# Block sums of the down projection's weights staged through DRAM, and thirteen pairs of k-tiles by Strassen's scheme

## Chip, cores and metric

One core of one Trainium2 chip runs the whole layer as one program. The metric is the device time of one execution in microseconds (us): 1745.18 us, the median of three runs of the kernel before (1744.41 to 1745.37).

## What is computed

A layer of depth 1 over 256 tokens of width 2048, in float32: a norm, a wide input projection, three branches (a gated convolution, a chunked linear recurrence, attention to 256 memory rows), an output projection with residual, and a feed-forward part. The change concerns the last matrix product:

```python
act = gelu(causal_dwconv3(up_g, conv_ffn_w) + conv_ffn_b) * up_v     # 256 x 5632
ffn_out = einsum('bsf,fd->bsd', act, w_ffn_down)                     # 5632 x 2048
x = x + rms_norm(ffn_out, norm_ffn_post)
```

## The kernel before

Every float32 operand is split in a rounded part and a rest (`wh` and `wl` of a weight, two halves of an activation tile), and a product is made of three matmuls: high by high, high by low, low by high. Weights come in tiles of 128 x 2048 (1 MiB) that SP's queue loads into three buffers named `w`. A tile is worked in units of 1024 columns, here called halves. For each, ScalarE casts `wh` (L1025, in the down projection L820) and VectorE subtracts to get `wl` (L1026, L821); there are four buffers of each. The main loop (L1118) walks about 600 units in order: the first 16 are the lead tiles, which carry the memory rows beside weights, then the key and value weights of the memory (`wkvT`, `wkvN`), then the input projection (`winT`, `winN`), the branches, `wout`, the up projection, the down projection. It prepares up to three units ahead and calls `bg(1)`, one step of background work, per unit. The instructions are then ordered by a list scheduler with its own idea of when an engine is free, except where `pin` or a raised priority holds them, so an instruction may stand on its engine far from its unit.

The down projection (`down_units`, `column_pair`) goes through two pairs of 512-column groups (p = 0 and 1), each over 22 pairs of k-tiles j. An ordinary pair, E below, takes 8 products in two units (`run_eight`). A pair in `SEVEN`, S below, takes 7 products by Strassen's scheme in Winograd's form in four units (`run_seven`): it needs sums of blocks of the activations, made in the up projection (`sums_of_operand`), and sums of blocks of the weights, which VectorE makes for every such pair (L840, L842, L843 in `load_seven`) in a quarter of the tile `down`. Ten of 22 pairs are S, alternating with E. `combine` folds the shared products at the last S of a column pair, and `run_shares` adds them to the accumulators for p = 1. `down` is 32 KB per partition, takes the memory of `a_x1` once the up projection is over, and also holds the results of p = 0 and the row of the last norm.

Of the kernel before, what the change touches and what calls it, by code (L numbers as in the profile page):

```python
# [16 lines left out]
P = 128  # L17
# [13 lines left out]
SEVEN = tuple(range(1, 20, 2))  # L31
FF = 4
# [29 lines left out]
def block_kernel(ctx: ExitStack, tc: tile.TileContext, xT, lead, cols, wkvT, wkvN, winT, winN, wbr, wout, wup, wlead, wdown, grow, xN, masks, out):  # L62
# [6 lines left out]
    psm = ctx.enter_context(tc.tile_pool(name="psm", bufs=4, space=bass.MemoryType.PSUM))  # L69
    phase1 = ExitStack()  # L70
# [469 lines left out]
    def mix_done(cg):  # L540
        def f(ps, tt):
# [6 lines left out]
            if tt == 0:  # L548
                st["x1"] = outer.tile([P, 2, D], F32, name="x1", tag="c16")
                st["a_x1"] = outer.tile([P, KT, 2 * T], F32R, name="a_x1", tag="a32")  # L550
# [153 lines left out]
    def sums_of_operand(j, y1, y2):  # L704
# [9 lines left out]
        a = st["act", 2 * j]  # L714
        p, q = t256("s12"), t256("s34")
        a11, a21, a12, a22 = y1[:, 0:P], y1[:, P:T], y2[:, 0:P], y2[:, P:T]
        nc.vector.tensor_tensor(p[:, 0:P], a21, a22, op=ALU.add)
        nc.vector.tensor_tensor(p[:, P:T], p[:, 0:P], a11, op=ALU.subtract)
        nc.vector.tensor_tensor(q[:, 0:P], a11, a21, op=ALU.subtract)
# [4 lines left out]

    def down_tile():
        if "down" not in st:
            st["down"] = outer.tile([P, 4, D], F32, name="down", tag="a32")
            st["ffn"], st["gf"] = st["down"][:, 0:2], st["down"][:, 2]
            nc.gpsimd.dma_start(st["gf"], grow[1].partition_broadcast(P))
# [6 lines left out]

    def down_norm(ps, tt, cg, n):
        down_tile()
        f, sums, w = st["ffn"][:, tt, cg * 512:(cg + 1) * 512], st["s3"][:, tt], st["s3w"][:, tt]
        with tc.high_priority():  # L740
            nc.scalar.activation(f, ps, AF.Square, accum_out=sums[:, n:n + 1])
            nc.vector.tensor_tensor(f, ps, st["gf"][:, cg * 512:(cg + 1) * 512], op=ALU.mult)
# [4 lines left out]
    def down_last(ps, tt, cg):  # L747
# [3 lines left out]
        x1, ffn = st["x1b"], st["ffn"][:, tt]  # L751
        hold = pin if tt else lambda op: op
        with tc.high_priority():
# [4 lines left out]
            hold(nc.scalar.activation(ffn[:, cut(cg)], ps, AF.Square, accum_out=sums[:, 3:4]))  # L758
# [3 lines left out]
            hold(nc.vector.tensor_tensor(ffn[:, cut(cg)], ps, st["gf"][:, cut(cg)], op=ALU.mult))  # L762
            hold(nc.vector.tensor_scalar(h, h, r, r, op0=ALU.mult, op1=ALU.mult))
            hold(nc.vector.tensor_scalar(r1, h, 1.5, r, op0=ALU.add, op1=ALU.mult))
            if tt:
                dg = t256("dg")[:, 0:P]
                hold(nc.scalar.activation(dg, ident, AF.Copy, scale=r1))
                hold(nc.tensor.matmul(turned, lhsT=dg, rhs=ffn[:, cut(0)], start=False, stop=True))
# [4 lines left out]
            for c, lo, hi in parts:  # L773
                f = ffn[:, c * 512 + lo:c * 512 + hi]
# [3 lines left out]

    def down_units():
        rest = [j for j in range(DP) if j not in SEVEN]
        mixed = []
        for n in range(10):
            mixed += [(rest[n], False), (SEVEN[n], True)]
        orders = [mixed + [(j, False) for j in rest[10:]]]
        mixed = []
        for n in range(9):
            mixed += [(rest[n], False), (SEVEN[n], True)] + ([(SEVEN[9], True)] if n == 4 else [])
        orders.append(mixed + [(j, False) for j in rest[9:]])  # L790
# [5 lines left out]
    def column_pair(p, order):  # L796
# [15 lines left out]
        def fetch(hold, j):  # L812
            hold["w"] = wpool.tile([P, 2048], F32, name="w", tag="w", bufs=3)
            nc.sync.dma_start(hold["w"], wdown[p * DP + j])
# [8 lines left out]
        def load_eight(hold, j, h):  # L823
            if h == 0:
                fetch(hold, j)
# [4 lines left out]
        def load_seven(hold, j, q):  # L830
            if q == 0:
                fetch(hold, j)
            w = hold["w"]
            if q < 2:
                wh, wl, low = halve(w[:, 1024:2048] if q == 0 else w[:, 0:512])
                low()
                return wh, wl
            t13, t24 = down_tile()[:, 3, 0:1024], down_tile()[:, 3, 1024:2048]
            if q == 2:
                nc.vector.tensor_tensor(t13, w[:, 512:1536], w[:, 0:1024], op=ALU.subtract)  # L840
                wh, wl, low = halve(t13)
                nc.vector.tensor_tensor(t24[:, 0:512], w[:, 1024:1536], t13[:, 0:512], op=ALU.subtract)  # L842
                nc.vector.tensor_tensor(t24[:, 512:1024], w[:, 1536:2048], t24[:, 0:512], op=ALU.subtract)  # L843
                low()
                return wh, wl
            wh, wl, low = halve(t24)
            low()
            return wh, wl
# [4 lines left out]
        def share(b):  # L853
            return st["down"][:, 3, shares[b] * 512:(shares[b] + 1) * 512]

        def load_shares(h):
            wh, wl, low = halve(st["down"][:, 3, h * 1024:(h + 1) * 1024])
# [8 lines left out]
        def combine():  # L866
            u = st["down"][:, 3].rearrange("p (a b) -> p a b", a=4)
            with tc.high_priority():
                nc.scalar.copy(u[:, 0], bank["P6"])
                nc.vector.tensor_tensor(u[:, 0], bank["P1"], u[:, 0], op=ALU.add)  # L870
                nc.scalar.copy(u[:, 1], bank["P7"])
                nc.vector.tensor_tensor(u[:, 1], u[:, 0], u[:, 1], op=ALU.add)
                nc.scalar.copy(u[:, 3], bank["P1"])
                nc.scalar.copy(u[:, 2], bank["P5"])
                nc.vector.tensor_tensor(u[:, 0], u[:, 0], u[:, 2], op=ALU.add)
                nc.vector.tensor_tensor(u[:, 2], u[:, 1], u[:, 2], op=ALU.add)
# [321 lines left out]
```

## Time and profile before

| what | value |
|---|---|
| median of the runs | 1745.18 us |
| the profiled execution | 1745.41 us, its span 1743.6 us |
| TensorE (PE) busy | 1734.7 us, 99% of the span |
| VectorE (DVE) busy | 1317.4 us, 76% |
| ScalarE (ACT) busy | 955.4 us, 55% |
| moved by DMA | 331.62 MB, mean 190 GB/s |

The profiled execution took 1745.41 us; its span, from the first to the last instruction seen, is 1743.6 us, so 1.8 us lie around it. The granted clock of TensorE is full over the whole span. Busy time of PE is modelled, since matmuls overlap; how close PE is to its limit is better read from the number of matmuls in a stretch.

### The profile page before, as it was taken

To read this page: it belongs to the slowest core of one execution; us is meant where nothing else is said; L and a number is where in the kernel's file an instruction comes from. 1 tells how busy PE (TensorE), PEld (TensorE's weight loads), DVE (VectorE), ACT (ScalarE), POOL (GpSimd) and SP (SyncE) were. 2 spreads that over 40 slices of the span, in tenths; PEclk is the share of its full clock that TensorE was granted. 3 is DMA by queue.
4 is the path that set the end of the run, shared out by engine and by line. 5 is a ranking of instruction groups with operands and counts; after the bars stand their busy time and mean duration, and the time that the engine had idled before them with its cause. 6 is when DMAs were issued, how large, how long until landed. Compare 5 with 4: busy or idle time off the path is not lost.

```text
span 1743.6 us, 24264 instructions
## 1 busy us (share of the span) xinstructions
PE 1734.7 (99%) x9354; PEld 1492.5 (86%) x9354; DVE 1317.4 (76%) x2149; ACT 955.4 (55%) x1505; POOL 8.4 (0%) x20
## 2 busy tenths in 40 slices
PE   9999999999999999999999999999999999999998
PEld 8888888888888888888888888888888888878786
DVE  8866665477788887867675587777777777888997
ACT  7644654456555465656664474444454444556554
POOL 0000000000000000000000000000000000000000
PEclk9999999999999999999999999999999999999999
DMA  8644455554454544465555555555555555555653
GB/s 312 234 173 154 160 193 193 188 174 170 171 180 168 183 169 170 172 241 191 193 191 176 188 214 182 186 192 192 181 186 190 193 181 184 214 197 198 245 196 131
DMA packets 47843, 331.62 MB, mean 190 GB/s; under 512 B 5488, under 2 KB 6000, under 8 KB 8432
## 3 DMA queue, kind: packets, MB, share of 16 engines
q1 hardware_dynamic: 45792, 321.28, 51.5%
q0 software_dynamic: 1504, 8.39, 1.3%
q8 instruction: 73, 1.20, 0.3%
q10 hardware_dynamic: 432, 0.41, 0.1%
q14 instruction: 42, 0.34, 0.1%
HBM read 325.87 MB, written 4.19 MB: 189 GB/s over the span
## 4 chain that ended last, share of the span: by engine, by line
PE 97%; DVE 1%; DMA 1%; ACT 1%; issue 0%; SPq 0%; ACTq 0%; DVEq 0%
PE acc L1083 47%; PE acc L1084 24%; PE acc L1096 3%; PE acc L1094 3%; PE acc L1095 3%; PE sm L808 2%; PE acc L808 2%; PE sm L809 2%; PE acc L807 2%; PE acc L809 2%; PE sm L807 2%; PE sm L397 1%; PE sm L1083 1%; DVE wl L821 0%; DMA w<-wdown 0%; PE sm L302 0%
## 5 line engine op out<-in xcount | busy, mean ns | idle before, releaser
L1083 PE MATMUL acc<-a_x,wh 128*128 128x512 f32 x3072 | 1088.3, 395 | 0.9 <-DVE a_x L94 0.9
L1025 ACT CAST wh<-w 128x1024 fp32r<-128x1024 f32 (+2 forms) x517 | 539.2, 1044 | 619.0 <-PE acc L1083 367.5
L1026 DVE TENSOR_TENSOR wl<-w,wh 128x1024 fp32r<-128x1024 f32 (+2 forms) x517 | 627.1, 1213 | 321.9 <-ACT wh L1025 320.3
L1084 PE MATMUL acc<-a_x,wl 128*128 128x256 f32 x3072 | 869.9, 283 | 0.0
L1083 PEld LDWEIGHTS acc<-a_x,wh 128*128 128x128 f32 x3072 | 577.1, 188 | 131.6 <-DVE a_x L94 1.5
L1084 PEld LDWEIGHTS acc<-a_x,wl 128*128 128x128 f32 x3072 | 577.7, 188 | 0.3
L112 DVE TENSOR_TENSOR ev<-acc,ev 128x256 f32<-128x256 f32 x245 | 102.3, 418 | 0.8 <-ACT ev L111 0.8
L820 ACT CAST wh<-w 128x1024 fp32r<-128x1024 f32 x88 | 81.6, 954 | 23.3 <-PE sm L809 10.5
L821 DVE TENSOR_TENSOR wl<-w,wh 128x1024 fp32r<-128x1024 f32 x88 | 91.8, 1097 | 2.7 <-ACT wh L820 2.7
L111 ACT COPY ev<-acc 128x256 f32<-128x256 f32 x245 | 88.2, 361 | 1.4 <-PE acc L1084 1.4
L820 ACT CAST wh<-down 128x1024 fp32r<-128x1024 f32 x42 | 44.0, 1051 | 75.4 <-PE sm L809 36.9
L821 DVE TENSOR_TENSOR wl<-down,wh 128x1024 fp32r<-128x1024 f32 x42 | 51.3, 1223 | 17.1 <-ACT wh L820 16.8
L808 PE MATMUL sm<-wl,act 128*128 128x512 f32 x136 | 53.7, 395 | 0.2 <-DVE wl L821 0.2
L808 PE MATMUL acc<-wl,act 128*128 128x512 f32 x136 | 53.8, 396 | 0.0
L809 PE MATMUL sm<-wh,act 128*128 128x512 f32 x136 | 53.7, 395 | 0.0
L807 PE MATMUL acc<-wh,act 128*128 128x512 f32 x136 | 53.7, 395 | 0.0
L807 PE MATMUL sm<-wh,act 128*128 128x512 f32 x136 | 53.6, 394 | 0.0
L809 PE MATMUL acc<-wh,act 128*128 128x512 f32 x136 | 53.6, 394 | 0.0
L1096 PE MATMUL acc<-wh,a_m 128*128 128x512 f32 x128 | 50.5, 395 | 0.0
L1094 PE MATMUL acc<-wh,a_m 128*128 128x512 f32 x128 | 50.5, 395 | 0.0
L1095 PE MATMUL acc<-wl,a_m 128*128 128x512 f32 x128 | 50.5, 395 | 0.0
L1083 PE MATMUL acc<-ya,wh 128*128 128x512 f32 x128 | 46.1, 398 | 0.0
(328 smaller groups left out, 1987.7 us busy)
## 6 DMA issues: line engine op xcount, KB each, us to landing
w<-winT SPq DMA_DIRECT2D x104, 1024.0 KB, 4.8
w<-wup SPq DMA_DIRECT2D x84, 1024.0 KB, 4.8
w<-wdown SPq DMA_DIRECT2D x44, 1024.0 KB, 4.9
w<-wbr SPq DMA_DIRECT2D x24, 1024.0 KB, 4.8
w<-wout SPq DMA_DIRECT2D x16, 1024.0 KB, 4.8
w<-wkvN SPq DMA_DIRECT2D x8, 1024.0 KB, 4.8
w<-winN SPq DMA_DIRECT2D x8, 1024.0 KB, 4.8
w<-lead SPq DMA_DIRECT2D x7, 1024.0 KB, 5.2
```

The source lines that it names most:

```text
L807: nc.tensor.matmul(ps, lhsT=hi, rhs=w0_, start=b not in started, stop=False)
L808: nc.tensor.matmul(ps, lhsT=hi, rhs=w1_, start=False, stop=False)
L809: nc.tensor.matmul(ps, lhsT=lo, rhs=w0_, start=False, stop=stop)
L820: nc.scalar.copy(wh[:, 0:n], src)
L821: return wh, wl, lambda: nc.vector.tensor_tensor(wl[:, 0:n], src, wh[:, 0:n], op=ALU.subtract)
L1025: ops = (nc.scalar.copy(wh[:, cs], wsl[:, cs]), nc.vector.tensor_tensor(wl[:, cs], wsl[:, cs], wh[:, cs], op=ALU.subtract))
L1026: nc.vector.tensor_tensor(wl[:, cs], wsl[:, cs], wh[:, cs], op=ALU.subtract))
L1083: hold(nc.tensor.matmul(job.ps, lhsT=wh[:, sl], rhs=a, start=first, stop=False))
L1084: hold(nc.tensor.matmul(job.ps[:, 0:T], lhsT=wl[:, sl], rhs=a[:, 0:T], start=False, stop=last))
L1094: nc.tensor.matmul(job.ps[tt], lhsT=hi, rhs=w0_, start=kt == 0, stop=False)
L1095: nc.tensor.matmul(job.ps[tt], lhsT=hi, rhs=w1_, start=False, stop=False)
L1096: nc.tensor.matmul(job.ps[tt], lhsT=lo, rhs=w0_, start=False, stop=kt == job.nkt - 1)
```

## The change

Thirteen pairs of k-tiles instead of ten go by the scheme of seven products: j = 14, 16 and 18 (`EXTRA`) join, and `PATTERN` sets the order of E and S in each column pair. The weight sums are no longer made in the down projection. A background generator `stage` loads each of the 26 weight tiles concerned (13 pairs, two column pairs) in the first half of the program on POOL's queue, adds blocks in place on DVE (one instruction of 1024 columns, two of 512) and stores the tile, which holds three sums, to a DRAM scratch `stored`, again on POOL's queue. Two buffers serve it. It is advanced by one step at each of the units 36 to 115 and 252 to 331. In the down projection an S pair loads three quarters of its weight tile and the whole stored tile. A smaller `down` (8 KB per partition) serves as a fourth weight buffer, in turn with the three of `w`. The block sums of the activations of the three new pairs are made at the first ordinary pairs of p = 0 (`late_sums`). Signs in the scheme and the order of its units change with the new sums; the results and the norm's row lie in pieces of 1024 columns, the second pieces allotted after `combine` of p = 1.

```diff
-        start_norm("x", "a32", outer)
+        start_norm("x", "a32", apool)
...
+    def late_sums(n):
+        j, down = EXTRA[n], down_tile()
+        x = st["sums"][n]
+        a1, a2 = st["act", 2 * j], st["act", 2 * j + 1]
+        y1, y2 = t256("s1"), t256("s2")
+        for y, a in ((y1, a1), (y2, a2)):
+            nc.vector.tensor_tensor(y, a[:, 0:T], a[:, T:2 * T], op=ALU.add)
+        st["xs", j] = x
+        block_sums(x, a1, y1, y2)
...
+    def stage(groups):
+        tiles = {}
+        def load_(n):
+            if n < len(groups):
+                p, j = groups[n]
+                tiles[n] = ph.tile([P, 2048], F32, name="stage", tag="stage", bufs=2)
+                nc.gpsimd.dma_start(tiles[n], wdown[p * DP + j])
+        load_(0)
+        yield
+        for n, (p, j) in enumerate(groups):
+            load_(n + 1)
+            yield
+            t = tiles.pop(n)
+            nc.vector.tensor_tensor(t[:, 0:1024], t[:, 0:1024], t[:, 512:1536], op=ALU.add)
+            yield
+            for c in (1024, 1536):
+                low = 0 if c == 1024 else 1024
+                nc.vector.tensor_tensor(t[:, c:c + 512], t[:, c:c + 512], t[:, low:low + 512], op=ALU.add)
+            yield
+            stored[p, j] = dram.tile([P, 2048], F32, name=f"sums{p}_{j}")
+            nc.gpsimd.dma_start(stored[p, j], t)
+            yield
...
+        def weight_tile(pos):
+            counter["w"] += 1
+            if counter["w"] % 4 == 0 and (pos < 20 if p == 0 else 1 < pos < 18):
+                return down_tile()
+            return wpool.tile([P, 2048], F32, name="w", tag="w", bufs=3)
+
+        def fetch(hold, pos, j, seven):
+            hold["w"] = weight_tile(pos)
+            src = wdown[p * DP + j]
+            if not seven:
+                nc.sync.dma_start(hold["w"], src)
+                return
+            for cs in (slice(0, 512), slice(1024, 2048)):
+                nc.sync.dma_start(hold["w"][:, cs], src[:, cs])
+            hold["sums"] = weight_tile(pos)
+            nc.sync.dma_start(hold["sums"], stored[p, j])
...
-            if q == 2:
-                nc.vector.tensor_tensor(t13, w[:, 512:1536], w[:, 0:1024], op=ALU.subtract)
-                wh, wl, low = halve(t13)
-                nc.vector.tensor_tensor(t24[:, 0:512], w[:, 1024:1536], t13[:, 0:512], op=ALU.subtract)
-                nc.vector.tensor_tensor(t24[:, 512:1024], w[:, 1536:2048], t24[:, 0:512], op=ALU.subtract)
-                low()
-                return wh, wl
-            wh, wl, low = halve(t24)
+            w, sums = hold["w"], hold["sums"]
+            wh, wl, low = halve((w[:, 0:512], w[:, 1024:2048], sums[:, 0:1024], sums[:, 1024:2048])[q])
             low()
...
@@ -1121,6 +1189,8 @@
         multiply(n)
         load_to(n + 3)
         bg(1)
+        if any(n in r for r in STAGE):
+            next(staging[0], None)
```

Where the scheduler puts this is seen in the order of the instructions on each engine. The first place is the start of the program. On POOL, whose queue does all of the staging (`ident` is a constant), before:

```order
masks.py:197 MEMSET ident 128x128
masks.py:199 ISA
masks.py:199 AFFINE_SELECT ident<-ident 128x128
L536 DMA gp<-grow 128x2048
L538 DMA xn<-xN 128x2048 x2
```

and with the change:

```order
masks.py:197 MEMSET ident 128x128
L824 DMA stage<-wdown 128x2048
masks.py:199 ISA
masks.py:199 AFFINE_SELECT ident<-ident 128x128
L824 DMA stage<-wdown 128x2048
L839 DMA sums_1_1128<-stage 128x2048
L824 DMA stage<-wdown 128x2048
```

The first two loads, 1 MiB each, wait for nothing and stand at the very start, not at unit 36. On DVE at the same place (`a_mem` is the memory operand, `lb` constants of the recurrence), before:

```order
L245 TENSOR_TENSOR lb<-lb_e_1006 128x8
L246 TENSOR_SCALAR lb<-lb 128x8
L94 SCALAR_TENSOR_TENSOR a_mem<-w,col_sb,a_mem 128x256
L248 TENSOR_SCALAR one_m_lb<-lb 128x8
L250 TENSOR_SCALAR la<-lb 128x8
L1026 TENSOR_TENSOR wl<-w,wh 128x768
```

and with the change:

```order
L251 TENSOR_TENSOR lb<-lb_e_1013 128x8
L832 TENSOR_TENSOR stage<-stage 128x1024
L100 SCALAR_TENSOR_TENSOR a_mem<-w,col_sb,a_mem 128x256
L1094 TENSOR_TENSOR wl<-w,wh 128x768
L252 TENSOR_SCALAR lb<-lb 128x8
L836 TENSOR_TENSOR stage<-stage 128x512
L254 TENSOR_SCALAR one_m_lb<-lb 128x8
L256 TENSOR_SCALAR la<-lb 128x8
L836 TENSOR_TENSOR stage<-stage 128x512
```

The three adds of the first staged tile now stand around the work of the second lead unit, the first of them ahead of its operand.

The second place is DVE at the end of the lead units, where the statistics of the memory's norm (`sqacc`) and the first evictions (`ev`) come together. Before:

```order
L207 TENSOR_TENSOR sqacc<-msq 128x256
L1026 TENSOR_TENSOR wl<-w,wh 128x768
L102 TENSOR_SCALAR sqacc<-sm 128x256
L1026 TENSOR_TENSOR wl<-w,wh 128x1024
L104 TENSOR_TENSOR sqacc<-sqacc,rs_mem 128x256
```

and with the change:

```order
L213 TENSOR_TENSOR sqacc<-msq 128x256
L836 TENSOR_TENSOR stage<-stage 128x512
L832 TENSOR_TENSOR stage<-stage 128x1024
L108 TENSOR_SCALAR sqacc<-sm 128x256
L1094 TENSOR_TENSOR wl<-w,wh 128x1024
L836 TENSOR_TENSOR stage<-stage 128x512
L1094 TENSOR_TENSOR wl<-w,wh 128x1024
L110 TENSOR_TENSOR sqacc<-sqacc,rs_mem 128x256
```

Three adds of the second and third staged tiles stand in it now. From there on the staging is dense: all adds of the fourth to the 26th tile stand between the 34th and the 98th `wl` half of the main loop, where the code asks for a tile per four units and for a second stretch from unit 252.

The third place is SP's queue at the start of the down projection, with the change (before, it is one load of `w<-wdown` 128x2048 per pair):

```order
L886 DMA w<-wdown 128x2048
L889 DMA w<-wdown 128x512
L889 DMA w<-wdown 128x1024
L891 DMA w<-sums_1_1128 128x2048
L891 DMA w<-sums_3_1262 128x2048
L889 DMA down<-wdown 128x512
L889 DMA down<-wdown 128x1024
L886 DMA w<-wdown 128x2048
```

An S pair now takes two tiles and three loads, 1.75 MiB, and every fourth tile is `down`.

## Rows read from the trace of the kernel before

**Rows 1.** The page, parts 1 and 4: engine totals, and the chain by engine.

```profile
PE 1734.7 (99%) x9354; PEld 1492.5 (86%) x9354; DVE 1317.4 (76%) x2149; ACT 955.4 (55%) x1505; POOL 8.4 (0%) x20
...
PE 97%; DVE 1%; DMA 1%; ACT 1%; issue 0%; SPq 0%; ACTq 0%; DVEq 0%
```

**Rows 2.** Waits of PE in the down projection: us in total, times, longest.

```profile
PE sm L807 <- ACT wh L820: 0.2, 1, 0.2
PE sm L808 <- DVE wl L821: 0.2, 1, 0.2
```

**Rows 3.** Windows, down projection: length; each engine's busy us (instructions); clock, DMA share, GB/s.

```profile
1640.00:1720.00 80.00, 80.00 (x346) 64.63 (x345) 70.16 (x73) 45.22 (x49) 2.15 (x4) 1.00 0.57 211
1500.50:1614.00 113.50, 113.30 (x487) 91.33 (x486) 96.98 (x102) 64.89 (x71) 0.54 (x1) 1.00 0.56 206
```

**Rows 4.** Groups by line, 1490 to 1744 us: count, busy us, mean ns, idle before.

```profile
L820 ACT CAST wh<-w 128x1024 fp32r<-128x1024 f32 x68 | 69.3, 1052 | 15.2 <-PE sm L809 6.8 <-PE acc L809 3.2 <-issue 2.7
...
L840 DVE TENSOR_TENSOR down<-w 128x1024 f32<-128x1024 f32 x20 | 24.5, 1224 | 7.9 <-DMA w<-wdown 7.7
L842 DVE TENSOR_TENSOR down<-w,down 128x512 f32<-128x512 f32 x20 | 13.8, 690 | 0.5
```

**Rows 5.** Windows, the start; columns as in Rows 3.

```profile
2.70:13.00 10.30, 10.11 (x52) 8.34 (x51) 6.97 (x21) 7.11 (x17) 0.00 (x0) 1.00 1.00 380
13.00:48.00 35.00, 34.87 (x199) 30.24 (x198) 32.36 (x62) 29.45 (x57) 0.00 (x0) 1.00 0.88 312
```

**Rows 6.** DMA issues, 0 to 13 us: count, KB each, median us to landing.

```profile
w<-lead SPq DMA_DIRECT2D x3, 1024.0 KB, 7.5
```

**Rows 7.** Timeline of DVE, 7.3 to 11 us: start, length, instruction, idle before.

```profile
7.71 0.48 DVE L94 SCALAR_TENSOR_TENSOR a_mem<-w,col_sb,a_mem 128x256 fp32r<-128x256 f32 x1 [0.23 <-ACT a_mem L93]
...
8.44 0.96 DVE L1026 TENSOR_TENSOR wl<-w,wh 128x768 fp32r<-128x768 f32 x1
...
10.18 0.48 DVE L94 SCALAR_TENSOR_TENSOR a_mem<-w,col_sb,a_mem 128x256 fp32r<-128x256 f32 x1 [0.49 <-ACT a_mem L93]
10.89 0.96 DVE L1026 TENSOR_TENSOR wl<-w,wh 128x768 fp32r<-128x768 f32 x1 [0.24 <-ACT wh L1025]
```

**Rows 8.** Timeline of PE at 9.5 us: start, length, instruction.

```profile
9.50 0.58 PE L1084 MATMUL acc<-a_mem,wl 128*128 128x256 f32 x3
```

**Rows 9.** Timeline of DVE at 46.7 us.

```profile
46.72 1.22 DVE L1026 TENSOR_TENSOR wl<-w,wh 128x1024 fp32r<-128x1024 f32 x1
```

**Rows 10.** Timeline of PE at 48 us.

```profile
48.06 0.32 PE L1084 MATMUL acc<-a_mem,wl 128*128 128x256 f32 x1
```

**Rows 11.** Windows, the staged stretch and two short ones; columns as in Rows 3.

```profile
83.50:278.00 194.50, 194.43 (x1121) 169.71 (x1120) 122.96 (x198) 101.08 (x158) 0.00 (x0) 1.00 0.49 173
...
778.00:784.00 6.00, 6.00 (x36) 5.27 (x35) 3.28 (x5) 2.76 (x5) 0.00 (x0) 1.00 1.01 423
1016.00:1022.00 6.00, 6.00 (x39) 5.21 (x37) 4.13 (x16) 5.76 (x15) 0.82 (x2) 1.00 1.02 427
```

**Rows 12.** Windows of L1026 alone, the same stretch: DVE busy (halves), clock, DMA.

```profile
83.50:278.00 194.50, 77.96 (x64) 1.00 0.49 173
```

**Rows 13.** Waits of DVE, 80 to 290 us, the longest.

```profile
DVE wl L1026 <- ACT wh L1025: 62.6, 53, 2.0
```

**Rows 14.** DMA issues of the whole span; columns as in Rows 6.

```profile
w<-wdown SPq DMA_DIRECT2D x44, 1024.0 KB, 4.9
...
xn<-xN POOLq DMA_DIRECT2D x2, 1024.0 KB, 6.6
out<-x POOLq DMA_DIRECT2D x2, 1024.0 KB, 5.9
...
gp<-grow POOLq DMA_DIRECT2D x1, 1024.0 KB, 5.3
```

**Rows 15.** DMA issues, 740 to 760 us, beside the load of gp.

```profile
w<-wbr SPq DMA_DIRECT2D x1, 1024.0 KB, 7.3
```

**Rows 16.** The page, part 3: SP's DMA queue, packets, MB, share of 16 engines.

```profile
q1 hardware_dynamic: 45792, 321.28, 51.5%
```

More of the change, by code (lines that the diff above doesn't have):

```diff
@@ L31 @@
 SEVEN = tuple(range(1, 20, 2))
+EXTRA = (14, 16, 18)
+PATTERN = ("ESSESSESSESSESSESSESEE", "ESSESSESSESSESSESSSEEE")
+STAGE = (range(36, 116), range(252, 332))
 FF = 4
@@ L723, in sums_of_operand @@
         split_into(a[:, P:T], a[:, T + P:2 * T], q[:, P:T])
+    def late_sums(n):
[7 more added lines that the diff above has]
+        block_sums(x, a1, y1, y2)
     def down_tile():
         if "down" not in st:
-            st["down"] = outer.tile([P, 4, D], F32, name="down", tag="a32")
-            st["ffn"], st["gf"] = st["down"][:, 0:2], st["down"][:, 2]
-            nc.gpsimd.dma_start(st["gf"], grow[1].partition_broadcast(P))
+            operands.close()
+            dp = ctx.enter_context(tc.tile_pool(name="dp", bufs=1, side="right"))
+            st["ffn"] = [[dp.tile([P, 1024], F32, name=f"ffn{t}{h}", tag=f"ffn{t}{h}") if h == 0 else None for h in range(2)] for t in range(2)]
+            st["gf"] = [dp.tile([P, 1024], F32, name=f"gf{h}", tag=f"gf{h}") if h == 0 else None for h in range(2)]
+            st["down"] = dp.tile([P, D], F32, name="down", tag="down")
+            st["sums"] = [dp.tile([P, 6 * P], F32R, name=f"xs{n}", tag=n) for n in ("ffn01", "ffn11", "gf1")]
+            st["dp"] = dp
+            row_piece(0)
             tc.keep_in_program_order(nc.scalar.preload_act_table_set("natural_log_exp_and_others"))
@@ L735, in down_tile, with row_piece, column @@
         return st["down"]
+    def row_piece(h):
+        cs = slice(h * 1024, (h + 1) * 1024)
+        if h:
+            st["gf"][1] = st["dp"].tile([P, 1024], F32, name="gf1", tag="gf1")
+            for t in range(2):
+                st["ffn"][t][1] = st["dp"].tile([P, 1024], F32, name=f"ffn{t}1", tag=f"ffn{t}1")
+        nc.gpsimd.dma_start(st["gf"][h], grow[1, cs].partition_broadcast(P))
+    def column(tiles, c):
+        return tiles[c // 2][:, c % 2 * 512:c % 2 * 512 + 512]
     def down_norm(ps, tt, cg, n):
         down_tile()
-        f, sums, w = st["ffn"][:, tt, cg * 512:(cg + 1) * 512], st["s3"][:, tt], st["s3w"][:, tt]
+        f, sums, w = column(st["ffn"][tt], cg), st["s3"][:, tt], st["s3w"][:, tt]
         with tc.high_priority():
             nc.scalar.activation(f, ps, AF.Square, accum_out=sums[:, n:n + 1])
-            nc.vector.tensor_tensor(f, ps, st["gf"][:, cg * 512:(cg + 1) * 512], op=ALU.mult)
+            nc.vector.tensor_tensor(f, ps, column(st["gf"], cg), op=ALU.mult)
             if n == 2:
@@ L773, in down_last @@
             for c, lo, hi in parts:
-                f = ffn[:, c * 512 + lo:c * 512 + hi]
+                f = ffn(c)[:, lo:hi]
                 hold(nc.vector.scalar_tensor_tensor(f, f, r1, x1[tt, c][:, lo:hi], op0=ALU.mult, op1=ALU.add))
                 nc.sync.dma_start(out[tt, :, c * 512 + lo:c * 512 + hi], f)
-    def down_units():
[L782 to L790, printed above, removed]
+    stored, staging = {}, []
+    def stage(groups):
[20 more added lines that the diff above has]
+            yield
+    counter = {"w": 0}
+    def down_units():
+        few = [j for j in range(DP) if j not in SEVEN + EXTRA]
+        many = list(SEVEN + EXTRA)
+        orders = []
+        for pattern in PATTERN:
+            e, s7 = iter(few), iter(many)
+            orders.append([(next(s7), True) if c == "S" else (next(e), False) for c in pattern])
+        staging.append(stage([(p, j) for p, order in enumerate(orders) for j, seven in order if seven]))
         made = []
@@ L893, in run_eight @@
                     one(1, b, c)
-            if p == 1 and h == 1 and pos in (0, 2, 4, 6):
-                if pos == 0:
+            nth = sum(not seven for _, seven in order[:pos])
+            if p == 0 and h == 1 and 0 < nth <= len(EXTRA):
+                late_sums(nth - 1)
+            if p == 1 and h == 1 and nth < 4:
+                if nth == 0:
                     st["x1b"] = {}
                 for n in range(2):
-                    tt, c = pos // 4, (pos // 2 % 2) * 2 + n
+                    tt, c = nth // 2, nth % 2 * 2 + n
                     x = st["fp"].tile([P, 512], F32, name=f"x1b{tt}{c}", tag=f"act{2 * j + n}")
```

68 lines of the change are left out of this document (32 added, 36 removed).

## The prediction

> **What bounds the kernel now.** I read the page first. PE is busy 99% of the span, and the chain that ended last is PE for 97% [rows 1]. The list of waits says the same of the down projection, the stage the change rewrites: PE waits there 0.4 us for a cast or a rest [rows 2]. The windows give the price of its work: 346 matmuls start in 80 us, 0.231 us each, at the full granted clock [rows 3]. So time falls only by fewer matmuls, and rises wherever another engine or a transfer keeps a weight half from PE. That needs a lead, which the timelines show. In the first 13 us there is none: DVE writes the rest of the second lead half from 8.44 to 9.40 and PE reads it at 9.50 [rows 7, 8]. There is none again at 48 us: a rest is finished at 47.94 and read at 48.06 [rows 9, 10]. Elsewhere DVE is held back by buffers: it waits 62.6 us, in 53 pieces, for casts [rows 13] that wait for PE to free one of four buffers. There I put its lead at 6 us, two halves of about 3 us (64 halves in 194.5 us [rows 12]).
>
> **What is removed.** In matmuls, each column pair had 10 x 7 + 12 x 8 = 166 products and will have 13 x 7 + 9 x 8 = 163. Three products of three matmuls, twice, are 18 matmuls: 18 x 0.231 = **-4.2 us**, all on the path. The sums in the down projection go: 20 x (1.224 + 2 x 0.690) = 52 us of DVE [rows 4]. But PE waits only 0.4 us there, so this is worth **-0.4** and no more. The copies and adds of `combine` that change, the table load, the split row of the norm and the residual rows moved to other pairs are a few us beside at least two E pairs, 11 us of later products, and are put at nothing. If that cover failed, the end of p = 0 would wait 1 to 2 us.
>
> **What is added, the start.** Program order says unit 36; the engines' order says otherwise. POOL's first two staged loads stand at the very start, and DVE's first add precedes the operand of the second lead unit. From 2.7 to 13 us the DMA engines are already full, share 1.00 at 380 GB/s [rows 5], and three lead tiles take 7.5 us to land [rows 6]. Two staged tiles are 2.10 MB, at that rate 5.5 us. If they went wholly ahead of the lead tile of units 2 and 3, PE would lose 5.5 us. If the lead is not delayed at all, DVE still has 2.6 us of new adds (1.224 + 2 x 0.690 by the same shapes, [rows 4]) ahead of that tile, against idle gaps of 0.23 + 0.49 + 0.24 us [rows 7] and about 0.3 of constants moved behind: 1.3 us. Queues that share evenly let about half of the staged bytes pass first, 2.8 us, with the adds mostly inside that wait. I take **+3.0**, from 1.3 to 5.5, near the row of the full DMA engines.
>
> Between 13 and 48 us DVE is idle 35.0 - 32.36 = 2.6 us [rows 5]. Four adds come in ahead of the half read at 48.06: 1.224 + 0.690 + 1.224 + 0.690 = 3.8 us, while two operand rests (0.48 each by [rows 7]) move behind it, so 2.8 net. If all idle time takes them in, 0.2; if none, 2.8. Much of that idle time lies after the first of the four adds has been absorbed by a grown lead, but before the dense run of work. I take **+2.0**.
>
> **The staged stretch.** The order puts 23 of 26 tiles between the 34th and the 98th half, which before took from 83.5 to 278 us, 194.5 us [rows 12]; a tile per 8.5 us, not per four units.
> - DVE: busy 123.0 us [rows 11] + 23 x 2.6 = 182.8 of 194.5, 94%. It fits, with 12 us left for waits that before were 62.6 [rows 13].
> - DMA engines: weights 173 GB/s x 194.5 us = 33.6 MB, staging 46 x 1.049 = 48.2 MB, together 81.9 MB or 421 GB/s. The fullest rows, with POOL's transfers beside SP's, are 423 and 427 GB/s at share 1.01 and 1.02 [rows 11]. At 427 it takes 191.8 us and costs nothing; at 380 [rows 5], 215.5, so 21.0 over, less 6 of lead: 15. At 400 it takes 204.8: 10.3 over, less 6, is 4.3.
> - The loop of a buffer: store 5.9, load 5.3 to 6.6 [rows 14], three adds with two rests between them 2.6 + 2.4 = 5.0, so 16.2 to 17.5 us per two tiles, against 16.9 given. DVE takes instructions in order, so when an add waits for its load, the rests behind it wait, and PE behind them. POOL's queue is in order too: a load waits for the store of the same buffer, and the next store waits behind that load. SP's weights keep their place, but each load may take 7.3 us instead of 4.9 when POOL's runs beside it [rows 14, 15]; the third buffer covers that.
>
> I take **+4.5**, from 0 to 15: a chain of loads and stores in turn doesn't keep the engines at their fullest row for 195 us.
>
> The Trainium skill bears on the rate. "SBUF — State Buffer", section "Summary: rules for kernel authors", says to count about 358 GB/s, the bound of HBM, for a transfer between HBM and SBUF; "HBM Reference", section "Specifications (TRN2)", adds that this is a core's share and that a core alone gets more. The rows of 423 and 427 go against the first for short stretches; by it the stretch would take 228.8 us, the rival below.
>
> **The down projection.** An S pair moves 1.75 MiB in 7 x 3 x 0.231 = 4.9 us, and a group E S S 4.5 MiB in 22 x 0.694 = 15.3 us, 309 GB/s, against 206 and 211 before [rows 3]; it is below the full rows. Four buffers serve five tiles, so a buffer has 4 x 15.3 / 5 = 12.2 us. It needs a load of 4.9 to 7.3 [rows 14, 15] and about 5.1 from landing to its last rest (2.8 between halves, 1.05 for a cast [rows 4], 1.22 for a rest [rows 9]): 10.0 to 12.4. DVE has 2.4 + 2 x 4.4 = 11.2 us of rests in such a group, with the late sums (about 2.9 us, an estimate from the 0.48 of a 256-column operand [rows 7]) 14.1 of 15.3: hidden, without much left. Two waits are new. The first load into `down` waits for the up projection's last matmul, with the next pair's load behind it on SP; it is wanted 15 x 0.694 - 2.3 = 8.1 us later and takes 4.9 to 7.3. At the start of p = 1, `down` is free only after the results of p = 0, four times two instructions of 512 columns at 0.69 [rows 4], 5.5 us; with 4.9 to 7.3 of load it lands at 10.4 to 12.8, wanted at 18 x 0.694 - 2.3 = 10.2. I take **+0.5**, from 0 to 8.
>
> **Sum.** -4.2 - 0.4 + 3.0 + 2.0 + 4.5 + 0.5 = +5.4 on the profiled execution's own time of 1745.4 us: **1750.8 us**, 0.3% slower. That execution is 0.2 us above the median, so nothing is corrected.
>
> **Rivals.**
> - **All but hidden, faster.** POOL's first tile lands within the 5.3 us of an undisturbed row [rows 14], before DVE's constants of the recurrence are through, and the lead tiles keep their landing. The start then costs 1.3 or less, the place at 48 us 0.2, and together some 0.9: 1745.4 - 4.6 + 0.9 = 1741.7. The point is whether the lead tile of units 2 and 3 still lands before its operand's 10.18 us [rows 7]. Against it: the share of 1.00 there [rows 5].
> - **The start alone is paid.** The staged stretch hides: -4.6 + 3.0 + 2.0 + 0.5, 1746.3. For it: 421 is just under 423, and the lead of 6 us; also DVE's 94%. Against: both limits at once.
> - **The mixed rate is lower.** Over the whole span SP's queue moved 321.28 MB in 51.5% of 1743.6 us, 358 GB/s per full share [rows 16]. At that rate the stretch takes 228.8, 34.3 over, less 6: 28.3 in place of 4.5, 1774.6. Against: rows 11. The Trainium skill's rule named above gives the same.
> - **The down projection waits for loads.** If loads take 8 us beside each other, each buffer's turn is 0.9 short, in some 17 groups, with the late `down` at p = 1 on top, less a small lead: 8 us more, 1759.
> - **It doesn't do what it says**: the spread over units 36 to 331 isn't in the program, as the order shows. That is part of the forecast.
>
> **Chances.** Forecast 0.38, the start alone 0.26, all but hidden 0.16, the down projection 0.12, the lower rate 0.08. A measurement of this kernel tells about 0.2%, 3.5 us, from no change. Faster than 1741.7: 0.14, from the first rival; within: 0.28 (the second, and what is left of the first); slower: 0.58. The range leaves out the lower half of the first rival and the lower rate: 1741.0 to 1765.0.
>
> **What would show it.** In the changed kernel's trace: PE's second lead unit starts 1 to 3 us late, with DVE waiting for a staged load before it and lead tiles landing after more than 9 us; the rest read at 48 us comes about 5 us late; between 80 and 290 us DVE is over 90% busy and has waits for `stage`, DMA's share is near 1, and PE has gaps; the down projection has 978 matmuls of products at 0.231 us, some 4 us less, and no wait for `w` over 1 us. I am wrong if PE's first lead units are on time, or if the staged stretch shows a DMA share well under 0.9 and no wait of DVE for a load, or if the down projection is longer than before.

## The result, and the profile after

The changed kernel takes 1833.12 us, the median of four runs (1827.12 to 1836.56), against 1745.05 of the kernel before: the ratio is 1.0501, with a 95% interval of 1.0472 to 1.0531. It is 88 us slower. I had forecast 5 us slower; the direction was right, the size was not.

The profiled execution took 1836.56 us, with a span of 1834.7. The page's totals (busy us, share, instructions), the strips by 40 slices (the granted clock, the DMA engines' share and their rate) and the chain:

```profile
PE 1758.2 (96%) x9336; PEld 1503.7 (82%) x9336; DVE 1343.7 (73%) x2206; ACT 961.5 (52%) x1522; POOL 36.8 (2%) x73
...
PEclk9998988999999999999999999999999999999999
DMA  9787778865454444445655546555555555688895
GB/s 357 284 317 277 292 256 291 302 218 197 164 178 169 178 167 179 164 181 206 228 186 184 188 165 224 188 191 188 188 184 184 184 185 185 209 308 295 300 330 195
...
PE 80%; issue 11%; DMA 5%; DVE 3%; POOL 1%; ACT 1%; SPq 0%; POOLq 0%; DVEq 0%; ACTq 0%
```

PE has 18 matmuls fewer, as it should, but its part of the chain falls from 97% to 80% [rows 1]. The clock, full everywhere before, falls below 0.9 in the fourth, the sixth and the seventh of the 40 slices. That points at the first 370 us. How much is lost, and where, is read by counting PE's matmuls in the two timelines and comparing the start of the one with the same number:

| up to | later than before, us |
|---|---|
| the 50th matmul (12 us before) | 4.1 |
| the 400th (80 us) | 7.0 |
| the 1600th (290 us) | 92.0 |
| the down projection's first product (1500.6 us) | 94.1 |
| the end of the span | 91.1 |

The losses are 4.1 and 2.9 us ahead of the staged stretch, **85.0 in it**, 2.1 crept in over the following 1200 us, and from the down projection's first product to the end 3.1 come back. Windows of the changed kernel, in the columns of [rows 3]: the whole staged stretch, 80 us of the down projection, and the start.

```profile
80.00:372.00 292.00, 231.19 (x1181) 196.98 (x1180) 183.56 (x281) 107.31 (x166) 24.63 (x46) 0.90 0.79 285
1734.10:1814.10 80.00, 80.00 (x346) 64.79 (x345) 58.60 (x56) 50.13 (x55) 2.68 (x5) 1.00 0.84 311
...
2.70:13.00 10.30, 7.14 (x34) 5.92 (x33) 5.72 (x16) 3.54 (x8) 0.14 (x1) 0.94 1.03 418
13.00:48.00 35.00, 32.90 (x183) 28.62 (x182) 32.20 (x56) 26.21 (x50) 1.61 (x3) 0.97 0.95 364
```

In the staged stretch PE is busy 231 of 292 us at a mean clock of 0.90 (with levels of 2.4 and 1.2 GHz, a fifth of the time at the lower), DVE 184 us, 63%, and the DMA engines have a share of 0.79 at 285 GB/s. No engine is full. Of the 85 us that are lost PE stands for 61 (292.0 - 231.2); the rest is in its busy time, at the lower mean clock. In the down projection 346 matmuls start in 80 us, as before [rows 3]; there PE is never short of work.

Who waits there? Waits of DVE, PE and POOL from 80 to 372 us (us in total, times, the longest):

```profile
DVE stage L832 <- DMA stage<-wdown: 92.5, 19, 7.9
DVE wl L1094 <- ACT wh L1093: 11.2, 12, 1.6
```

```profile
PE acc L1152 <- DVE wl L1094: 29.9, 9, 6.1
PE sm L319 <- DVE p L316: 25.0, 6, 7.5
```

```profile
POOL stage L824 <- DMA sums<-stage: 213.0, 22, 13.5
```

DVE stands 92.5 us before its first add of a tile, for the staged load. Its easy waits for casts, 62.6 us before [rows 13], have shrunk to 11.2: the lead is gone. PE waits for rests and for the attention's `p` that stand behind the add in DVE's order. And POOL stands 213 us with a load in hand that waits for a store to land. The timeline of POOL from 215 to 250 us (start, length, instruction, idle time before it and what ended it) shows how:

```profile
217.89 0.53 POOL L824 DMA_DIRECT2D stage<-wdown  x1 [8.73 <-DMA sums<-stage]
218.51 0.55 POOL L839 DMA_DIRECT2D sums<-stage  x1
232.08 0.53 POOL L824 DMA_DIRECT2D stage<-wdown  x1 [13.03 <-DMA sums<-stage]
232.69 0.54 POOL L839 DMA_DIRECT2D sums<-stage  x1
243.72 0.53 POOL L824 DMA_DIRECT2D stage<-wdown  x1 [10.49 <-DMA sums<-stage]
244.34 0.54 POOL L839 DMA_DIRECT2D sums<-stage  x1
```

A load waits for the store before it; the next store, whose sums are ready, stands behind that load and goes out 0.6 us after it. So load and store run together, and the next load waits for this store. From 130 to 358 us every store goes out 0.6 to 3.2 us after a load; where it is 1.5 us or more, the store still waited for DVE. A tile then costs one store to its landing and this gap: the 19 loads from 130.5 to 357.8 us are 12.6 us apart. The page's DMA issues (count, KB each, median us to landing) give the price, against 5.3 to 6.6 and 5.9 us in [rows 14]:

```profile
stage<-wdown POOLq DMA_DIRECT2D x26, 1024.0 KB, 8.2
sums<-stage POOLq DMA_DIRECT2D x26, 1024.0 KB, 10.4
```

The fourth tile's first add is at 89.3 us and the 26th's at 365.8: 12.57 us a tile, where DVE's order asks for one each 194.5 / 23 = 8.46 us [rows 12]. Over 22 tiles that is 90 us, less the lead of 6: 84, near the 85 that were lost. The slower clock of PE is hardly a cause of its own here: DVE's work and its waits for staged loads fill 276 of the 292 us, and it waits only 11 for casts.

### The profile page after: what moved, and what is told of

Read it like the earlier page. It is cut to its first block, busy times and chain, and to the rows that moved or that the text cites. A ratio compares the mean times of both kernels' runs of the same rounds, so it can differ in the third digit from the quotient of the medians.

```text
span 1834.7 us, 24551 instructions
## 1 busy us (share of the span) xinstructions
PE 1758.2 (96%) x9336; PEld 1503.7 (82%) x9336; DVE 1343.7 (73%) x2206; ACT 961.5 (52%) x1522; POOL 36.8 (2%) x73
## 4 chain that ended last, share of the span: by engine, by line
PE 80%; issue 11%; DMA 5%; DVE 3%; POOL 1%; ACT 1%; SPq 0%; POOLq 0%; DVEq 0%; ACTq 0%
PE acc L1151 38%; PE acc L1152 20%; DMA stage<-wdown 4%; PE acc L1164 2%; PE acc L1163 2%; PE acc L1162 2%; PE sm L871 2%; PE sm L873 2%; PE sm L872 2%; PE acc L872 2%; PE acc L871 2%; PE acc L873 2%; PE sm L403 1%; DVE wl L1094 1%; DVE stage L836 1%
## 5 line engine op out<-in xcount | busy, mean ns | idle before, releaser
L1151 PE MATMUL acc<-a_x,wh 128*128 128x512 f32 x3072 | 1108.3, 402 | 0.9 <-DVE a_x L100 0.9
L1151 PEld LDWEIGHTS acc<-a_x,wh 128*128 128x128 f32 x3072 | 586.2, 191 | 140.3 <-DVE a_x L100 1.4
L1152 PEld LDWEIGHTS acc<-a_x,wl 128*128 128x128 f32 x3072 | 588.5, 192 | 33.2 <-DVE wl L1094 32.8
L898 DVE TENSOR_TENSOR wl<-w,wh 128x1024 fp32r<-128x1024 f32 (+1 forms) x110 | 121.5, 1130 | 43.8 <-ACT wh L897 43.5
L897 ACT CAST wh<-w 128x1024 fp32r<-128x1024 f32 (+1 forms) x110 | 105.4, 975 | 63.2 <-PE sm L873 28.2
L832 DVE TENSOR_TENSOR stage<-stage 128x1024 f32<-128x1024 f32 x26 | 31.8, 1223 | 93.6 <-DMA stage<-wdown 93.6
L871 PE MATMUL sm<-wh,act 128*128 128x512 f32 x124 | 48.9, 395 | 0.0
L873 PE MATMUL acc<-wh,act 128*128 128x512 f32 x124 | 48.9, 395 | 0.0
L873 PE MATMUL sm<-wh,act 128*128 128x512 f32 x124 | 48.9, 394 | 0.0
L871 PE MATMUL acc<-wh,act 128*128 128x512 f32 x124 | 48.6, 396 | 0.2 <-ACT wh L897 0.2
L1151 PE MATMUL acc<-ym,wh 128*128 128x512 f32 x128 | 45.4, 394 | 0.0
## 6 DMA issues: line engine op xcount, KB each, us to landing
sums<-stage POOLq DMA_DIRECT2D x26, 1024.0 KB, 10.4
```

The lines of the kernel that those rows point to most:

```text
L871: nc.tensor.matmul(ps, lhsT=hi, rhs=w0_, start=b not in started, stop=False)
L873: nc.tensor.matmul(ps, lhsT=lo, rhs=w0_, start=False, stop=stop)
L897: nc.scalar.copy(wh[:, 0:n], src)
L898: return wh, wl, lambda: nc.vector.tensor_tensor(wl[:, 0:n], src, wh[:, 0:n], op=ALU.subtract)
L1151: hold(nc.tensor.matmul(job.ps, lhsT=wh[:, sl], rhs=a, start=first, stop=False))
L1152: hold(nc.tensor.matmul(job.ps[:, 0:T], lhsT=wl[:, sl], rhs=a[:, 0:T], start=False, stop=last))
```

## The experiments

Four theories were set against each other. **A**: the loop of two buffers through POOL's one queue is longer than the pace at which DVE's order asks for tiles; DVE waits, and PE behind it. **B**: loads, stores and weights together are more bytes than the DMA engines move. **C**: DVE has no room for so many adds. **D**, added after the first four versions: the place of the operands in SBUF sets the pace of the matmuls. Each version is the changed kernel with the edits shown, unless it says otherwise.

**No staging at all.**

```diff
-        if any(n in r for r in STAGE):
-            next(staging[0], None)
...
-            nc.sync.dma_start(hold["sums"], stored[p, j])
+            nc.sync.dma_start(hold["sums"], src)
```

> The staging (loads, adds, stores of POOL and DVE) is left out, and each S pair loads its second tile straight from the down projection's weights: as many bytes on SP, the same casts, rests and matmuls; the block sums of the weights are not computed. All theories agree that what is left is the saving: 1745.4 - 4.2 - 0.4 + 0.5 = 1741.3 us, 1740 to 1744. If it is over 1750, the new down projection or its operand sums cost what I put on the staged stretch, and the theories below all lack their ground.

It took 1744.98 us, ratio 0.9999 (0.9989 to 1.0008). So the staging costs the 88 us, but the saving that all theories agreed on is missing. The timeline has it: from the up projection's end to the last product PE is 4.0 us shorter than before, but it reaches that point 3.05 us late, having lost 0.33 us in each 300 matmuls of the up projection, where no matmul was edited. In the trace of before, a pair of matmuls of 512 and 256 columns there starts 351.1 ns after the pair before it; in this one, and in the changed kernel, 353.3. This is where theory D comes from.

**The adds alone.**

```diff
+            if 1 < n < len(groups):
+                tiles[n] = tiles["kept", n % 2]
+            elif n < 2:
...
-            stored[p, j] = dram.tile([P, 2048], F32, name=f"sums{p}_{j}")
-            nc.gpsimd.dma_start(stored[p, j], t)
...
-            nc.sync.dma_start(hold["sums"], stored[p, j])
+            nc.sync.dma_start(hold["sums"], src)
```

> All 78 adds stay on DVE, but on two tiles that are loaded once; no tile is loaded again, none is stored, and the S pairs read the plain weights: the block sums are not what they should be. Theory A (the two buffers' loop through POOL's one queue keeps DVE waiting): the adds without transfers cost only the start, 1742 to 1749 us, and DVE waits for no staged load after 15 us. Theory B (the transfers are too many bytes for the DMA engines): the same, 1742 to 1749. Theory C (DVE has no room for 67 us of adds so close together): most of the 88 us stays, over 1790 us.

It took 1748.8 us, ratio 1.0022 (1.0013 to 1.0031). The window of the staged stretch:

```profile
80.00:372.00 292.00, 291.91 (x1600) 250.56 (x1599) 225.59 (x334) 148.62 (x221) 0.00 (x0) 1.00 0.51 179
```

DVE carries 226 us of work in 292 and PE doesn't stand; theory C falls. What is left against the version without staging, 3.8 us, is the start with its two staged loads: PE's 50th matmul is 4.05 us late here, its 275th (51 us) 4.8.

**Held in the order of the program, a tile per four halves.** The STAGE line is unchanged; every load, add and store of `stage` is wrapped in the call that keeps it at its place:

```diff
-                nc.gpsimd.dma_start(tiles[n], wdown[p * DP + j])
+                pin(nc.gpsimd.dma_start(tiles[n], wdown[p * DP + j]))
...
-            nc.gpsimd.dma_start(stored[p, j], t)
+            pin(nc.gpsimd.dma_start(stored[p, j], t))
```

> The loads, adds and stores are held in the order in which the program writes them, so a tile is staged per four weight halves (about 12 us) from the 36th half on, 20 in the first run and 6 in the second; nothing at the start. Theory A (a tile takes 10 to 14.6 us around the loop): the pace of 12 us is just what the loop gives, so waits for staged loads remain but PE loses far less: 1743 to 1770 us. Theory B (bytes): 20 x 2.10 MB and the weights in about 240 us are some 350 GB/s; if 358 or less is the limit, the loss stays at tens of us, if it is 423 there is none. Theory C: 2.6 of 12 us of DVE fits beside 62%, no loss, 1741 to 1744.

It took 1769.86 us, and its four runs lie far apart (1754.99, 1764.49, 1775.24, 1775.69); ratio 1.0129 (1.0077 to 1.0181). The window shows the loss, the timeline of POOL how it begins:

```profile
200.00:370.00 170.00, 156.21 (x797) 131.01 (x796) 111.50 (x147) 80.58 (x110) 13.31 (x25) 0.97 0.84 311
```

```profile
198.54 0.55 POOL L839 DMA_DIRECT2D sums<-stage  x1 [4.63 <-DVE stage L836]
206.16 0.53 POOL L824 DMA_DIRECT2D stage<-wdown  x1 [7.08 <-DMA sums<-stage]
209.72 0.54 POOL L839 DMA_DIRECT2D sums<-stage  x1 [3.03 <-DVE stage L836]
220.21 0.53 POOL L824 DMA_DIRECT2D stage<-wdown  x1 [9.95 <-DMA sums<-stage]
220.82 0.54 POOL L839 DMA_DIRECT2D sums<-stage  x1
232.31 0.53 POOL L824 DMA_DIRECT2D stage<-wdown  x1 [10.96 <-DMA sums<-stage]
232.93 0.54 POOL L839 DMA_DIRECT2D sums<-stage  x1
```

Up to 209.72 a store waits for its own add (the releaser is DVE), and goes out some us after the load. From 220.82 it has no wait of its own: it stood ready behind the load. Ahead of 206 us the stores land 5.1 to 8.0 us after their issue, from 220 to 370 us 10.6 to 15.0. The two transfers have locked onto each other, and in this profile they stay so up to the end of the first run of staging. Runs as different as 1755 and 1776 fit a lock that closes early or late; that was seen in one profile only.

**A tile per six halves.** This is the held version, with the STAGE line changed as well.

```diff
-STAGE = (range(36, 116), range(252, 332))
+STAGE = (range(36, 116, 3), range(37, 116, 3), range(252, 332, 3), range(253, 332, 3))
```

> As the version with four halves per tile, but with two steps in three halves: a tile per six halves, about 18 us, 13 in the first run and 13 in the second. Theory A: 18 us is more than the loop's 14.6, DVE hardly waits for a load, and the saving comes out: 1741 to 1744 us, which is faster than both kernels. Theory B: 13 x 2.10 MB per 230 us and the weights are 290 to 310 GB/s, hidden: the same. Both are wrong if PE still loses over 10 us here.

It took 1751.4 us, ratio 1.0035 (1.0022 to 1.0048). The staged stretch costs nothing any more: PE is 6.3 us late at its 75th matmul and 6.5 at its 700th. Loads and stores keep apart (one pair of 26 overlaps, for 2.7 us), and their issues read:

```profile
stage<-wdown POOLq DMA_DIRECT2D x26, 1024.0 KB, 6.1
sums<-stage POOLq DMA_DIRECT2D x26, 1024.0 KB, 4.9
```

The miss of 1741 to 1744 has two parts: 6.3 us at the start, and the pace of the up projection, as above. Holding the program's order doesn't hold the first two loads: POOL has nothing to do before them, so they still go out at 1.5 and 2.1 us, beside the lead tiles.

**The transfers alone.** The three add instructions of `stage` are taken out.

> All 26 loads and 26 stores of the staging are made, as in the changed kernel, but DVE's 78 adds are left out, so the stored tiles are the plain weights and the block sums are missing; DVE has no instruction that waits for a staged load. Theory A (DVE, in order, waits for the buffers' loop through POOL's queue, and PE behind it): the transfers alone cost only the start, 1748 to 1752 us, and a pair of loads and a pair of stores through the one queue show what the loop takes without DVE. Theory B (loads, stores and weights together are more than the DMA engines move, so weight tiles land late): PE waits for w through the casts, and most of the 88 us stays, over 1790 us.

It took 1773.52 us, ratio 1.0159 (1.0146 to 1.0172): more than A said, less than B. With no add to wait for, the 52 transfers ran from the first microsecond on, and PE lost 21.4 us by 51 us, among the lead tiles and the x operand (seven lead tiles of 1 MiB land after 11.5 us in the median, against 5.2 before), and 5 more by 135 us. After that:

```profile
120.00:240.00 120.00, 119.95 (x710) 104.68 (x709) 80.86 (x144) 62.12 (x104) 13.98 (x26) 1.00 1.00 397
```

For 120 us the DMA engines carry 397 GB/s of loads, stores and weights at a share of 1.00, and PE is never without work. A tile takes (234.1 - 24.7) / 22 = 9.5 us by its loads. So the engines' limit would have cost (9.5 - 8.46) x 22 - 6 = 17 us, near the 15 of my upper bound; the 285 GB/s of the changed kernel aren't that limit.

**Stores on SP.**

```diff
-            nc.gpsimd.dma_start(stored[p, j], t)
+            nc.sync.dma_start(stored[p, j], t)
```

> Only the queue of the 26 stores is changed: SP issues them, between its weight loads, so a store no longer stands behind a load that waits for the store before it. DVE has nearly the order of the changed kernel (the adds between the 34th and the 96th half). Theory A: the turn of a buffer falls from some 24 us per two tiles to the 16 to 18 of my sum, against 16.9 given, and the loss falls from 88 to under 40 us: 1750 to 1785 us. Theory B: as many bytes in as little time, so 1815 to 1840 as before. A third outcome, slower than the changed kernel, would mean that SP's weight loads now stand behind the adds.

It took 1801.01 us, ratio 1.0311 (1.0297 to 1.0325): 32 us better, and between the two forecasts.

```profile
80.00:372.00 292.00, 255.58 (x1336) 218.62 (x1335) 197.59 (x298) 123.32 (x186) 11.68 (x22) 0.93 0.86 312
```

```profile
DVE stage L832 <- DMA stage<-wdown: 58.0, 11, 9.6
```

A tile takes 11.07 us ((328.6 - 85.0) / 22), so 22 x 2.61 - 6 = 51 us, and 52.3 were lost. My 16 to 18 us for a turn took the transfers for undisturbed; here the loads land after 7.6 us (median) and the stores after 8.1, which with 5.0 of adds is 20.7. So the queue's order accounts for 33 of the 85 us. The other 52 are a loop whose transfers are slow beside each other; how much of that is the engines' limit (17 us by the estimate above) was not separated, and a third buffer, which would tell, was not tried. SP's weight loads now stand behind stores that wait for DVE, but that shows in one wait only, 3.9 us of ACT for a weight tile.

**Four halves per tile, stores on SP.** This is the same single edit, on the held version with a tile per four halves.

> The version with a tile per four halves, with one edit: its 26 stores are issued by SP. DVE's adds stand at the same halves. Theory A, sharpened by that version's trace (from 220 us on each store is issued 0.6 us behind a load that had waited for the store before; the two run together, the store takes 10 to 15 us, and the next load waits for it, so the two stay locked to each other): with the store no longer behind the waiting load the lock cannot form, a turn is 16 to 21 us against 24 given, and the loss of the staged stretch goes: 1747 to 1753 us, the start's 4 to 6 us and the operands' place among it. Theory B (bytes): as many bytes in the same time, 1760 to 1776 as before.

It took 1753.59 us, ratio 1.0046 (1.0029 to 1.0063), 16 us better than with the stores on POOL and 0.6 above the range of A. The window that lost time there, and DVE's wait from 100 to 370 us (51.0 us in 11 pieces there):

```profile
200.00:370.00 170.00, 170.00 (x907) 145.03 (x906) 128.34 (x169) 93.02 (x127) 6.87 (x13) 1.00 0.92 346
```

```profile
DVE stage L832 <- DMA stage<-wdown: 3.4, 5, 1.1
```

More GB/s than in the version that lost time, and no loss: B falls for this pace and A stands. The new queue doesn't make a store faster by itself: the stores take 8.3 us (median) on SP here, and took 5.1 to 8.0 on POOL before the lock. Of the 7.3 us that are left at PE's 1300th matmul, 6.6 are the start.

**The kernel before, with its operands on the right side.** This is the kernel before, with one pool added.

```diff
+    apool = ctx.enter_context(tc.tile_pool(name="apool", bufs=1, side="right"))
...
-        start_norm("x", "a32", outer)
+        start_norm("x", "a32", apool)
...
-                st["a_x1"] = outer.tile([P, KT, 2 * T], F32R, name="a_x1", tag="a32")
+                st["a_x1"] = apool.tile([P, KT, 2 * T], F32R, name="a_x1", tag="a32")
...
-            st["down"] = outer.tile([P, 4, D], F32, name="down", tag="a32")
+            st["down"] = apool.tile([P, 4, D], F32, name="down", tag="a32")
```

> The kernel before with one edit: the 32 KB operand tile (a_x, then a_x1, then down) lies in a pool of its own on the right side of SBUF, as in the change, so it and all pools behind it have the addresses of the change; no instruction is added. Theory D (the place of the operands in SBUF sets the pace of a pair of matmuls, 351.1 ns before and 353.3 in all versions with the change, in the up projection): 1747.5 to 1749 us, and pairs of 353.3. Rival (the pace comes from another part of the change): 1745.2, and 351.1.

Its profiled execution took 1748.37 us, the median of twelve is 1750.44, ratio 1.0021 (1.0009 to 1.0032). The pair of matmuls takes 353.3 ns. By windows of 430 us in the up projection, first the kernel before, then this one:

```profile
1050.00:1480.00 430.00, 430.00 (x2451) 376.88 (x2450) 335.03 (x567) 212.25 (x337) 0.00 (x0) 1.00 0.53 188
```

```profile
1050.00:1480.00 430.00, 430.00 (x2435) 373.41 (x2434) 333.36 (x565) 210.21 (x334) 0.00 (x0) 1.00 0.53 187
```

So 16 fewer matmuls start in the same time, at the same clock, with no wait. Theory D holds for the profiled execution; the median is 1.4 us above its range. The edit moves the pools behind the operand tile too, so which of the addresses matters isn't shown. Two of the twelve runs took 1741.7 and 1741.9 us, the other ten 1748.4 to 1752.0; what differed in the two isn't known, as no profile caught one.

**Six halves per tile, late first loads.** This is the version with six halves per tile, and a small write of DVE at the 36th half that holds the first two loads back.

```diff
+                if n < 2:
+                    pin(nc.vector.memset(tiles[n][:, 0:2], 0.0))
```

> The version with a tile per six halves, and the first two staged loads held back by a small write of DVE into their tiles at the 36th half, so that they no longer stand beside the lead tiles. If the start was all that this version lost against the one without staging, it comes to 1745.0 us (1744 to 1746.5), level with the kernel before. If it stays at 1750, the 6.3 us at the start had another cause than the two loads.

It took 1747.32 us, ratio 0.9997 (0.9983 to 1.0010). The start is mended: PE's 75th matmul is 0.4 us late instead of 6.3. The 2.3 us beyond the expected time are again the pace of the matmuls: PE is 5.5 us late at the up projection's end. Of that, 2.9 us are lost in the up projection, as in the version without staging. Some 2 us more come from a stretch ahead of it, and show that the place is not all that sets the pace: from the 4000th to the 5500th matmul, in the branches and the output projection, the kernel before takes 282.8 us. With its operands on the right it takes 281.1, and so do the version without staging and the one with six halves; this one, with the same pools as those two, takes 283.1. Its runs have two groups too, three at 1738.2 to 1738.3 us and nine at 1746.8 to 1748.1.

**The same, operands back at their place.** To the version just shown one edit is added: a_x and a_x1 become seven tiles (six of 4 KB per partition, one of 8) that follow each other in the first pool, under the tags that the down projection then uses.

```diff
+        self.tiles = {t: pool.tile([P, 4 if t == "down" else 2, 2 * T], F32R, name=name + t, tag=t) for t in dict.fromkeys(self.TAGS)}
...
-        start_norm("x", "a32", apool)
+        start_norm("x", None, outer)
...
-                st["a_x1"] = apool.tile([P, KT, 2 * T], F32R, name="a_x1", tag="a32")
+                st["a_x1"] = Parts(outer, "a_x1")
...
-            operands.close()
-            dp = ctx.enter_context(tc.tile_pool(name="dp", bufs=1, side="right"))
+            dp = outer
```

> The version with a tile per six halves and late first loads, with the operands a_x and a_x1 back at the place in SBUF that they have in the kernel before: seven tiles one after the other in the first pool, reused in the down projection, no pool on the right side. If the place sets the pace of the matmuls (theory D), the up projection goes back to 351.1 ns a pair, its 3 us come back, and the time is 1745.3 - 4.2 - 0.4 + 0.4 for the start + 0.5 = 1741.6 us, 1740.5 to 1743, faster than the kernel before and in one mode only. If it stays at 1745 to 1748, or has runs at 1738 and at 1747, the place is not what set the pace.

It took 1742.67 us (1741.53 to 1743.0 in eleven runs) against 1745.22: ratio 0.9985 (0.9976 to 0.9994). **It is faster than both kernels**, and leaves nothing out. The gain over the kernel before is small, 2.5 us, but its slowest run lies under the fastest of 21 of that kernel (1743.88). Its up projection and its staged loads and stores:

```profile
1050.00:1480.00 430.00, 430.00 (x2452) 376.86 (x2451) 335.13 (x567) 212.25 (x337) 0.00 (x0) 1.00 0.54 188
```

```profile
stage<-wdown POOLq DMA_DIRECT2D x26, 1024.0 KB, 5.7
...
sums<-stage POOLq DMA_DIRECT2D x26, 1024.0 KB, 4.9
```

The pace of before is back, with one group of runs.

**No staging, operands back at their place.** The two edits of the first version and the one just shown.

> The version without staging (S pairs read plain weights, the block sums are missing) with the operands back at the place of the kernel before. Theory D: 1745.3 - 4.0 = 1741.3 us, 1740.3 to 1742.5, against 1745.0 with the operands on the right side. Without theory D: 1745.0.

It took 1741.5 us, ratio 0.9981 (0.9972 to 0.9991). This is what the new down projection is worth by itself, 3.7 us; the staging, spread out, costs 1.2 of them.

## Why the prediction failed

- **The staged stretch: the step that failed.** I put +4.5, from 0 to 15; it was +85.0. The step was the loop of a buffer. I added a store of 5.9, a load of 5.3 to 6.6 and adds of 5.0 to 16.2 to 17.5 us per two tiles, and it took 25.1. I had taken both transfers from rows in which POOL moved one tile, or two of one kind, after a long rest [rows 14]. And I had seen that the next store stands behind the waiting load, but not what follows: the two then run together, 8.2 and 10.4 us, and stay so. With the stores on another queue 52 of the 85 us were still lost, at 7.6 and 8.1 us: the durations were too short even without the lock. A loop that is too long by 8 us in 17 loses that on every turn; the bound of 15 came from the bytes, and bytes don't bound a loop.
- **DVE and DMA engines there.** I expected DVE over 90% busy and a share near 1. They were 63% and 0.79. My own sign of error (a share well under 0.9) was met in half: DVE did wait for loads. The 421 GB/s that I asked of the engines were near what they gave without DVE's waits, 383 to 427 in windows of 20 us.
- **The rate.** The Trainium skill, "SBUF — State Buffer", section "Summary: rules for kernel authors", counts with 358 GB/s between HBM and SBUF. The version with the transfers alone moved 397 GB/s for 120 us, so here the rule doesn't bind; the rival that rested on it would have given 1774.6, and not for the reason that cost the time.
- **The start.** I put +3.0, from 1.3 to 5.5. It was 4.1: the three lead tiles landed after 11.4 us instead of 7.5 [rows 6], and PE waited 2.96 us before its second lead unit. At 48 us I put +2.0, from 0.2 to 2.8; it was 2.9, in two pieces.
- **The down projection.** I put -4.2, -0.4 and +0.5, together -4.1. By its products it was -4.0; the tail after the last product took 0.9 us more, so -3.1. Neither new wait showed: PE waits there 0.8 and 0.2 us for rests and casts. The rival in which it waits for loads did not come.
- **What I had at nothing.** The move of the operand tile to the right side of SBUF was in the diff, and I did not cost it. It is worth some 3 us in the up projection, most of the saving, which is why the version without staging only drew level.

## What to carry to other kernels

Before a second stream of transfers is put on a queue, write down the loop of its buffers with durations from a stretch in which the DMA engines are as full as they will be, and follow the queue's order: here a store that stood behind a load which waited for a store ran beside that load, turn after turn. Give such a loop a pace well above its turn (here 18 us a tile, so 36 for a turn of two tiles, which took 25 in the changed kernel; where loads and stores kept apart, it is 6.1 + 4.9 + 5.0 = 16), and hold the instructions where the program has them, with the first transfers held back by a dependence and not by their place alone. And after an edit of the pools, compare the pace of untouched matmuls.

## What was not expected of the hardware

- Addresses alone, of the operand tile and the pools behind it, changed the pace of TensorE: 353.3 against 351.1 ns per pair of matmuls at the full clock with no wait, 3 us in the up projection. In the branches and the output projection the same move gave 1.6 us back (281.1 against 282.8), and two versions with these pools took 283.1 there. Two kernels with the operands on the right side had, in twelve runs each, two and three that were some 9 us faster than the others; the two that ran ten times each (no staging, adds alone) had not, nor any with the old place. Why is open.
- A 1 MiB store took 4.9 us (median) when it ran apart from the queue's loads, and 10.4 in the changed kernel, where most were issued 0.6 to 3.2 us behind a load on the same queue, though the engines' share was only 0.79.
- Loads, stores and weights together kept 397 GB/s over 120 us without one late weight for PE.
